# A streaming encoder layer on one core: VectorE's half of every split queued one step after ScalarE's, the spread product two steps behind its packing, the first FFN group loaded later

## The chip, the core and the metric

The kernel runs as one program on one core of a Trainium2 chip. The metric is the device time of one execution in microseconds (us); less is better. Before the change it is 1680.91 us, the median of three runs (1679.38 to 1682.36).

## The reference, cut to what matters

The reference is one layer of a hybrid encoder over 320 frames (256 of a prompt, 64 of a running stream that has 256 cached frames):

```python
xn = rmsnorm(x, norm_mix)
q, k, v, u, vs, g = split(xn @ w_in)          # 8 heads of 128; u, vs 1024 each; g 4096
a  = stick_breaking(q, k, v)                  # log-sigmoid, reversed cumulative sum, exp, @ v
bb = gelu(u) * (w_spatial . rmsnorm(gelu(vs)) + b_spatial)      # "SGU"
merged = sigmoid(g_a + b) * (a @ w_branch_a) + sigmoid(g_b + b) * (bb @ w_branch_b)
h  = x + merged @ w_out
hn = rmsnorm(h, norm_ffn)
h  = h + (silu(hn @ w_gate) * (hn @ w_up)) @ w_down             # 5632 hidden features
return rmsnorm(h, norm_final), k, v, vs
```

Everything is float32, and the weights (256 MB in all) are read once. A float32 product is made out of three matmuls of a high and a low part: high by high, high by low, low by high.

## The kernel before, in words

Features lie on the 128 partitions and the 320 frames on the free axis. A weight block of 128 output features is taken in steps of eight k-blocks, 24 matmuls a step (`product`, L98 to L100). After each step the code calls `tick()`, which counts the step and then calls everything that was registered for it with `at(tick, fn, rank)`, in the order of the ranks. So the program order of each engine's queue is written out by hand: TensorE, VectorE, ScalarE and SyncE run exactly what was emitted, in that order (`manual_schedule`), and only GpSimd's order is left to the framework. An instruction of VectorE that waits holds up all that stands behind it in VectorE's queue, whoever needs that.

Weights come in two schemes.

- `Plain` (six of the q/k/v heads, the 16 blocks of `w_out`, the first three gate/up pairs of the FFN): SyncE loads half a block (L115), ScalarE rounds it to fp32r (`high`, L120), VectorE subtracts (`low`, L123). The step `s` has its high at `s - 2` and its low at `s - 1`. The tiles: `raw` to `w`.
- `Group` (all other weights, in fp16, two steps to a unit): SyncE loads the raw block (L322); the largest magnitude of its rows is bounded by ScalarE (`junk`, L199, sum of magnitudes) or by VectorE (`tops`, L195, largest magnitude); VectorE packs it (`packed`, L207); TensorE spreads it over all partitions with one small product (`row`, L211), into the only buffer of its kind; VectorE makes the power of two from it (`close`: `peak`, `down`, `up`, L215 to L217, and `undo`, L342); ScalarE makes the high half (`w`, L349) and VectorE the low half (L352). The product of a unit starts at step `s`; its load is emitted at `s - lead`, the bound at `s - lead + 3`, the high at `s - 3`, the low at `s - 2`; with `last` the load step of the group's last unit, the packing comes at `last + 4`, the spreading at `last + 5`, the closing at `last + 6`. `lead` is 10 up to the out projection and 14 in the FFN.

Raw weights have five buffers (`RAW`), and four more (`raw2`) once the FFN begins; the `w` tiles have three (`SPLIT`). The small activation tiles rotate through 51 slots (`slot`, tile names `S`, `half`, `gate`, `act`).

The stages, with their times in the profile before: the first two q, k and v heads, with their loads (to 55 us); twelve Plain steps, four heads, in which the normalized input is made besides: VectorE multiplies `x` by the norm's factor (`normed`, L294), ScalarE makes its fp16 high half (`half`, L160) and VectorE the low half (L161) (to about 102 us); the fp16 heads, with the attention of four pairs of heads beside them, its small steps spread over twenty steps per pair by `attend` (to 330 us); the SGU, the gates and the branch products (to 640 us); the out projection (to 767 us); the FFN, in three slices, the first twelve steps Plain, which run while the norm of `h` is made and `ffn.normed` prepares 16 tiles as above (`mg`, L294; `half`, L160, L161); and from 1668 us the final norm and the stores. For the FFN's activations `gated` multiplies gate and up (L1029 to L1036), for its residual `downed` adds.

Splits of other activations are written the same way, ScalarE's copy at once followed by VectorE's subtraction in the same step: `gained` (L153, L154), `parts` in the attention (L593, L594), `merge` behind the branch products, and the softmax-like part of the attention (`att_soft`, L654 to L656, which loads ScalarE's function tables).

Of the kernel before, what the change touches and what calls it, by code (L numbers as in the profile page):

```python
# [22 lines left out]
H = 8  # L23
# [24 lines left out]
def stream_step(ctx: ExitStack, tc: tile.TileContext, xT, w_in, w_a, w_b, w_out, w_gu, w_down,  # L48
# [33 lines left out]

    rooms = {}
# [67 lines left out]
    def gained(src, gain, home=slot):  # L151
        hi, lo = home(), home()
        nc.scalar.activation(out=hi, in_=src, func=AF.Copy, scale=gain)  # L153
        nc.vector.scalar_tensor_tensor(out=lo, in0=src, scalar=gain, in1=hi.bitcast(F32),  # L154
                                       op0=ALU.mult, op1=ALU.subtract)
        return hi, lo

    def half(src, factor):
        x = slot((2, T), F16, "half")
        nc.scalar.activation(out=x[:, 0], in_=src, func=AF.Copy, scale=factor)  # L160
        nc.vector.scalar_tensor_tensor(out=x[:, 1], in0=src, scalar=factor, in1=x[:, 0], op0=ALU.mult, op1=ALU.subtract)  # L161
# [113 lines left out]
    class Features:  # L275
# [16 lines left out]
        def normed(self, m, src, factor, home=None):  # L292
            t = src if home is None else home
            nc.vector.tensor_tensor(out=t, in0=src, in1=got[factor], op=ALU.mult)  # L294
# [293 lines left out]
    def parts(src, engine=None):  # L588
# [5 lines left out]
        (engine or nc.vector).tensor_tensor(out=view(lo), in0=src, in1=view(hi.bitcast(F32)), op=ALU.subtract)  # L594
# [5 lines left out]
    def att_parts(p):  # L600
# [8 lines left out]
        nc.vector.tensor_tensor(out=own[:, :, 1], in0=new, in1=own[:, :, 0].bitcast(F32), op=ALU.subtract)  # L609
# [21 lines left out]
    def att_gather(p, part):  # L631
        s = attn[p]
        if part == 0:
# [5 lines left out]
            for j, r in enumerate(ROWS):  # L639
                nc.vector.tensor_tensor(out=z[0][r, Z:], in0=zs[j][r, TS : TS + PAST], in1=low[r, TS:], op=ALU.add)  # L640
                nc.vector.tensor_tensor(out=z[1][r, Z:], in0=zs[j][r, 0:TS], in1=low[r, 0:TS], op=ALU.add)
            nc.vector.tensor_tensor(out=z[1][:, Z:], in0=z[1][:, Z:], in1=mown, op=ALU.add)
# [50 lines left out]
    def att_join(p, what):  # L693
        s = attn[p]
        t = s[what]
        if what == "vt":
            av = s["av"] = rooms["late"].tile([P, 5 * P], F32, tag="av", name="av")
            together(av, t[0])
            s["ap"] = parts(av[:, 0 : 4 * P].rearrange("p (j d) -> p j d", j=2)[:, :, 0:P])
        else:  # L700
# [3 lines left out]
            s["tp"] = [parts(wt[:, j * 5 * P : j * 5 * P + TP]) for j in range(2)]  # L704

    def att_out(p):
# [15 lines left out]
        a = [slot(dt=F32, name="aT") for _ in range(2)]  # L722
        nc.scalar.copy(out=a[0], in_=po[0][:, 0:T])
        nc.scalar.copy(out=a[1][:, 0:TP], in_=po[1][:, 0:TP])
        nc.scalar.copy(out=a[1][:, TP:T], in_=po[0][:, T : T + TS])
        for t in a:
            aT.add(t)

# [476 lines left out]
```

## Time and profile before

| | |
|---|---|
| three runs, median | 1680.91 us (1679.38 to 1682.36) |
| profiled execution, its own time | 1682.18 us |
| its span in the profile | 1680.4 us |
| TensorE clock granted, mean | 0.985 |
| PE busy | 1615.0 us, 96% of the span |
| VectorE (DVE) busy | 1095.5 us, 65% |
| ScalarE (ACT) busy | 1009.1 us, 60% |
| GpSimd (POOL) busy | 57.3 us, 3% |
| read from HBM | 256.03 MB, 156 GB/s over the span |

The profile is one execution, recorded by the hardware. In its rows PE is TensorE, DVE VectorE, ACT ScalarE, SPq the DMA issues of SyncE; "L123" is line 123 of the kernel; "w<-raw" is a tile written and the tile read; a bracket holds the idle time of the engine just before an instruction and the instruction that ended it. PEclk is the clock granted to TensorE, 1.00 being full speed. Times are from the start of the span.

### The profile page before, as it was taken

The numbers are of one execution on the slowest core, as the hardware profiler recorded it, in microseconds if no ns is written. First come the engines' busy times: TensorE is split into PE (matmuls) and PEld (weight loads), VectorE is DVE, ScalarE is ACT, GpSimd is POOL, SyncE is SP. The second block draws the span as 40 slices with busy tenths as digits, with TensorE's granted clock in tenths as the row PEclk, the third lists the DMA queues.
The fourth block names the chain that finished last, engine by engine and source line by source line (L and its number), as shares of the span: only waits on it lengthen the run. The fifth ranks groups of instructions, "written<-read, shape, count | busy, mean of one in ns | idle before, by whom it ended". The sixth has DMA issues, their size and how long they took to land.

```text
span 1680.4 us, 28045 instructions
## 1 busy us (share of the span) xinstructions
PE 1615.0 (96%) x11692; PEld 1235.4 (74%) x11692; DVE 1095.5 (65%) x1819; ACT 1009.1 (60%) x1119; POOL 57.3 (3%) x80
## 2 busy tenths in 40 slices
PE   9979898999999999998599999999999999999997
PEld 9967666677777778998567777777777777777775
DVE  6678776786665565555565568765565686655775
ACT  6468888768766762444455657445555664555652
POOL 0110101100000000111000000000000000000000
PEclk9989999999999999999899999999999999999999
DMA  8556753564544444554444444544444444443331
GB/s 307 169 156 181 197 169 118 161 178 151 176 151 166 161 157 144 171 172 141 148 168 167 151 151 154 197 152 151 152 170 176 154 151 158 168 176 126 113 113 64
DMA packets 100512, 268.35 MB, mean 160 GB/s; under 512 B 28992, under 2 KB 35392, under 8 KB 100384
## 3 DMA queue, kind: packets, MB, share of 16 engines
q1 hardware_dynamic: 97936, 261.36, 46.7%
q0 software_dynamic: 1312, 3.80, 0.7%
q8 instruction: 91, 1.49, 0.4%
q10 hardware_dynamic: 1136, 1.39, 0.2%
q14 instruction: 37, 0.30, 0.1%
HBM read 256.03 MB, written 5.51 MB: 156 GB/s over the span
## 4 chain that ended last, share of the span: by engine, by line
PE 83%; DVE 7%; ACT 7%; DMA 2%; issue 2%; SPq 0%; ACTq 0%; DVEq 0%
PE acc L98 26%; PE acc L99 26%; PE acc L100 26%; DVE w L352 2%; PE aux L444 2%; ACT junk L199 1%; ACT w L349 1%; DMA raw<-w_gu 1%; DVE w L123 1%; PE acc L444 1%; ACT half L160 1%; PE row L211 1%; DMA raw<-w_in 1%; DVE tops L195 0%; DVE half L161 0%
## 5 line engine op out<-in xcount | busy, mean ns | idle before, releaser
L99 PE MATMUL acc<-half,w 128*128 128x320 f16 x3232 | 969.3, 300 | 0.0
L98 PE MATMUL acc<-half,w 128*128 128x320 f16 x3232 | 969.3, 300 | 0.0
L100 PE MATMUL acc<-half,w 128*128 128x320 f16 x3232 | 969.1, 300 | 0.0
L349 ACT ACTIVATE w<-raw,up 128x2048 f16<-128x2048 f32 (+1 forms) x206 | 405.6, 1969 | 413.6 <-PE acc L100 398.2
L352 DVE SCALAR_TENSOR_TENSOR w<-raw,up,w 128x2048 f16<-128x2048 f32 (+1 forms) x206 | 475.2, 2307 | 55.6 <-ACT w L349 55.0
L98 PEld LDWEIGHTS <-w 128*128 128x128 f16 x3232 | 317.1, 98 | 125.0 <-issue 1.3
L100 PEld LDWEIGHTS <-w 128*128 128x128 f16 x3232 | 317.1, 98 | 124.1
L99 PEld LDWEIGHTS <-w 128*128 128x128 f16 x3232 | 317.1, 98 | 118.4
L199 ACT ACTIVATE junk<-raw 128x2048 uint8<-128x2048 f32 (+1 forms) x149 | 277.8, 1865 | 8.5 <-DMA raw<-w_gu 8.5
L1036 DVE TENSOR_TENSOR act<-bb,ev 128x320 f32<-128x320 f32 x44 | 21.6, 492 | 171.9 <-ACT bb L1034 168.9
L195 DVE TENSOR_REDUCE tops<-raw 128x1 f32<-128x2048 f32 (+1 forms) x57 | 127.7, 2241 | 3.2 <-DMA raw<-w_gu 3.2
L215 DVE TENSOR_REDUCE peak<-row 128x1 f32<-128x128 f32 x148 | 42.3, 286 | 133.7 <-PE row L211 133.6
L120 ACT CAST w<-raw 128x1024 fp32r<-128x1024 f32 x56 | 58.7, 1047 | 82.4 <-PE acc L100 70.1
L123 DVE TENSOR_TENSOR w<-raw,w 128x1024 fp32r<-128x1024 f32 x56 | 77.7, 1390 | 14.1 <-ACT w L120 14.1
L98 PE MATMUL acc<-mh,w 128*128 128x320 f32 x256 | 79.3, 310 | 0.0
L99 PE MATMUL acc<-ml,w 128*128 128x320 f32 x256 | 79.1, 309 | 0.0
L100 PE MATMUL acc<-mh,w 128*128 128x320 f32 x256 | 79.1, 309 | 0.0
L211 PE MATMUL row<-turner,packed 128*128 128x128 bf16 x148 | 32.8, 222 | 41.4 <-DVE packed L207 40.2
L100 PE MATMUL acc<-S,w 128*128 128x320 f32 x144 | 47.6, 331 | 13.2 <-DVE w L123 13.2
L211 PEld LDWEIGHTS <-packed 128*128 128x128 bf16 x148 | 14.5, 98 | 50.6 <-DVE packed L207 45.4
L98 PEld LDWEIGHTS acc<-mh,w 128*128 128x128 f32 x256 | 48.1, 188 | 0.0
L99 PEld LDWEIGHTS acc<-ml,w 128*128 128x128 f32 x256 | 48.1, 188 | 0.0
(226 smaller groups left out, 1279.3 us busy)
## 6 DMA issues: line engine op xcount, KB each, us to landing
raw<-w_gu SPq DMA_DIRECT2D x176, 512.0 KB, 5.6
raw<-w_in SPq DMA_DIRECT2D x141, 512.0 KB, 4.8
raw<-w_down SPq DMA_DIRECT2D x80, 512.0 KB, 5.0
raw<-w_out SPq DMA_DIRECT2D x32, 512.0 KB, 3.9
raw<-w_a SPq DMA_DIRECT2D x16, 512.0 KB, 3.7
raw<-w_b SPq DMA_DIRECT2D x16, 512.0 KB, 4.6
raw<-w_down SPq DMA_DIRECT2D x16, 256.0 KB, 5.0
x<-xT SPq DMA_DIRECT2D x8, 320.0 KB, 7.5
```

The source lines that it names most:

```text
L98: nc.tensor.matmul(ps[:, :T], a, x[0], start=first, stop=False, skip_group_check=True)
L99: nc.tensor.matmul(ps[:, :T], a, x[1], start=False, stop=False, skip_group_check=True)
L100: nc.tensor.matmul(ps[:, :T], b, x[0], start=False, stop=last, skip_group_check=True)
L120: nc.scalar.copy(out=self.w[j][0], in_=self.raw[:, j * HALF * P : (j + 1) * HALF * P])
L123: nc.vector.tensor_tensor(out=self.w[j][1], in0=self.raw[:, j * HALF * P : (j + 1) * HALF * P], in1=self.w[j][0].bitcast(F32), op=ALU.subt ...
L195: nc.vector.tensor_reduce(out=self.tops[:, i : i + 1], in_=src, axis=mybir.AxisListType.X, op=ALU.max, apply_absolute_value=True)
L199: nc.scalar.activation(out=junk, in_=src, func=AF.Abs, accum_out=self.tops[:, i : i + 1])
L211: nc.tensor.matmul(self.row[:, :P], self.own.to_broadcast([P, P]), turner, start=True, stop=True)
L215: nc.vector.tensor_reduce(out=top, in_=self.row[:, :P], axis=mybir.AxisListType.X, op=ALU.max)
L349: nc.scalar.activation(out=w[:, 0], in_=self.raw[u][:, : self.width[u]], func=AF.Copy, scale=self.scale.up)
L352: nc.vector.scalar_tensor_tensor(out=self.w[u][1], in0=self.raw.pop(u)[:, : self.width[u]], scalar=self.scale.up, in1=self.w[u][0], op0=AL ...
L444: nc.tensor.matmul(first[b][h][:, :T], w[:, (h * n + j) * P : (h * n + j + 1) * P], xs[c + j][i], start=not last and c + j + i == 0, stop= ...
```

## The change

It changes the order in which the same instructions stand in the queues, and a few buffers.

- A helper `after(n, fn)` registers `fn` for `n` steps later. VectorE's part of a split (`half`, `gained`, `parts`, the own queries in `att_parts`, the sums of `att_gather`) is emitted one step after ScalarE's part, and a ScalarE part that needs a VectorE result is emitted one step after that: the `half` behind `normed`, the `parts` behind `av` and `wt` in `att_join`, the split planes behind `sgu_gain`, the copies behind `att_out`, the high and low of `merge`, `residual`, `gated` and the squares of `downed`. The last ones of a stage (the last three of 16) keep the old way.
- In `Group` the spreading comes at `last + 6` and the closing at `last + 7`. With `lead` 11 in place of 10 before the FFN, the load, the bound and the packing of a group stand one step earlier against its products, and the spreading and the closing where they stood. In the FFN the lead stays 14, so there the spreading and the closing stand one step nearer to the products; the first FFN group has lead 12, since the lead may not reach to before the FFN's first step (`min(14, now - ffn_start)`), so its loads stand behind later Plain loads.
- `normed` in the FFN gets six buffers of its own in the late pool in place of the one `mg` buffer; `merge` writes into a gate's tile. The SGU's four pairs of groups come every three steps in place of 10/3, and the output of the attention one step later.

Each engine has the same instructions, in the same number, in both kernels. The core of the diff (L numbers move by 6 or 7 up to `Group`, and by 14 and more behind the attention):

```diff
+    def after(n, fn, *a, rank=5):
+        if n == 0:
+            fn(*a)
+        else:
+            at(state["tick"] + n, fn, *a, rank=rank)
...
     def half(src, factor):
         x = slot((2, T), F16, "half")
         nc.scalar.activation(out=x[:, 0], in_=src, func=AF.Copy, scale=factor)
-        nc.vector.scalar_tensor_tensor(out=x[:, 1], in0=src, scalar=factor, in1=x[:, 0], op0=ALU.mult, op1=ALU.subtract)
+        after(1, lambda: nc.vector.scalar_tensor_tensor(out=x[:, 1], in0=src, scalar=factor, in1=x[:, 0],
+                                                        op0=ALU.mult, op1=ALU.subtract), rank=3)
...
-            t = src if home is None else home
+            t = src if home is None else home()
             nc.vector.tensor_tensor(out=t, in0=src, in1=got[factor], op=ALU.mult)
-            self.half.append(half(t, self.gain[:, m : m + 1]))
+            after(1, lambda: self.half.append(half(t, self.gain[:, m : m + 1])), rank=3)
...
             last = start + 2 * len(units) - 2 - lead
-            assert last + 6 <= start - 3
+            assert last + 7 <= start - 3
             at(last + 4, lambda: self.scale.pack(), rank=3)
-            at(last + 5, lambda: self.scale.spread(), rank=1)
-            at(last + 6, self.close, late_undo, rank=1)
+            at(last + 6, lambda: self.scale.spread(), rank=1)
+            at(last + 7, self.close, late_undo, rank=1)
...
-        (engine or nc.vector).tensor_tensor(out=view(lo), in0=src, in1=view(hi.bitcast(F32)), op=ALU.subtract)
+        after(wait, lambda: (engine or nc.vector).tensor_tensor(out=view(lo), in0=src, in1=view(hi.bitcast(F32)), op=ALU.subtract))
...
-            s["ap"] = parts(av[:, 0 : 4 * P].rearrange("p (j d) -> p j d", j=2)[:, :, 0:P])
+            after(1, lambda: s.update(ap=parts(av[:, 0 : 4 * P].rearrange("p (j d) -> p j d", j=2)[:, :, 0:P])))
...
-                groups[kind, s, i] = Group([pieces(w_gu[i], 0, KD), pieces(w_gu[KF + i], 0, KD)], now, lambda: [ffn.undo], 14, (1,) if made % 2 else ())
+                groups[kind, s, i] = Group([pieces(w_gu[i], 0, KD), pieces(w_gu[KF + i], 0, KD)], now, lambda: [ffn.undo], min(14, now - ffn_start), (1,) if made % 2 else ())
...
-        at(base + 3 + m // 2, lambda m=m: ffn.normed(m, hs[m], "rh", t320("mg", 1)))
+        at(base + 3 + m // 2, lambda m=m: ffn.normed(m, hs[m], "rh", lambda: rooms["raw"].tile([P, T], F32, tag="normed", bufs=6, name="normed")))
```

How the queues change is seen at three places. The first is VectorE's queue in the twelve Plain steps; `x` is the input being normalized, `half` its fp16 halves, `w` the weights' low half, `k` a head. Before:

```order
L123 TENSOR_TENSOR w<-raw,w 128x1024
L743 TENSOR_TENSOR k<-acc,rx 128x320
L294 TENSOR_TENSOR x<-x,rx 128x320
L161 SCALAR_TENSOR_TENSOR half<-x,gain_608,half 128x320
L294 TENSOR_TENSOR x<-x,rx 128x320
L161 SCALAR_TENSOR_TENSOR half<-x,gain_608,half 128x320
L123 TENSOR_TENSOR w<-raw,w 128x1024
```

and in the changed kernel, from the same product of a `k` head on:

```order
L757 TENSOR_TENSOR k<-acc,rx 128x320
L301 TENSOR_TENSOR x<-x,rx 128x320 x2
L129 TENSOR_TENSOR w<-raw,w 128x1024
L167 SCALAR_TENSOR_TENSOR half<-x,gain_608,half 128x320 x2
L301 TENSOR_TENSOR x<-x,rx 128x320 x2
L129 TENSOR_TENSOR w<-raw,w 128x1024
```

The two `half` of a step no longer stand directly behind the `x` from which ScalarE has to make their high halves: there is a `w`, a step's worth of ScalarE's time, between them.

The second place is VectorE's queue at the beginning of the fp16 heads, where the attention's first `parts` (`S`) fall; `packed` is the packing of the next group. Before:

```order
L215 TENSOR_REDUCE peak<-row 128x1
L216 TENSOR_TENSOR down<-peak,bits 128x1
L217 TENSOR_TENSOR up<-down,bits 128x1
L342 TENSOR_SCALAR undo<-down,undo_610 128x1
L352 SCALAR_TENSOR_TENSOR w<-raw,up,w 128x2048
L207 TENSOR_SCALAR packed<-tops 128x1
L743 TENSOR_TENSOR v<-acc,rx 128x320
L215 TENSOR_REDUCE peak<-row 128x1
```

and in the changed kernel:

```order
L359 SCALAR_TENSOR_TENSOR w<-raw,up,w 128x2048
L601 TENSOR_TENSOR S<-q,S 128x256
L601 TENSOR_TENSOR S<-k,S 128x256 x2
L616 TENSOR_TENSOR S<-q,S 128x2x64
L757 TENSOR_TENSOR v<-acc,rx 128x320
L214 TENSOR_SCALAR packed<-tops 128x1
L222 TENSOR_REDUCE peak<-row 128x1
L223 TENSOR_TENSOR down<-peak,bits 128x1
```

In the kernel before, the `peak` behind a `packed` belongs to the same group, and the spreading product that reads `packed` stands in the very next step of TensorE's queue; in the changed kernel the `peak` is that of the group ahead, and the spreading product stands two steps behind its `packed`. The `S` have moved away from ScalarE's copies by a step as well.

The third place is SyncE's queue at the FFN's start, with the buffers' numbers; in the piece before, `raw_8504` and `raw_8575` are the two units of the first FFN group, `raw_8664` the first of the second, and `raw_8573` and `raw_8662` Plain blocks:

```order
L115 DMA raw_8502<-w_gu 128x1024
L322 DMA raw_8504<-w_gu 128x1024
L115 DMA raw_8573<-w_gu 128x1024
L322 DMA raw_8575<-w_gu 128x1024
L115 DMA raw_8662<-w_gu 128x1024
L322 DMA raw_8664<-w_gu 128x1024
```

and in the changed kernel, where `raw_8556`, `raw_8643` and `raw_8645` are these three units and `raw_8554` and `raw_8641` the Plain blocks:

```order
L121 DMA raw_8486<-w_gu 128x1024
L121 DMA raw_8554<-w_gu 128x1024
L329 DMA raw_8556<-w_gu 128x1024
L121 DMA raw_8641<-w_gu 128x1024
L329 DMA raw_8643<-w_gu 128x1024
L329 DMA raw_8645<-w_gu 128x1024
```

The first group's first unit stands one Plain block later against the Plain loads (beside `raw_8554`, the fifth of six blocks, where it stood beside `raw_8502`, the fourth), and the last Plain block stands ahead of that group's second unit, where it stood behind it.

More of the change, by code (lines that the diff above doesn't have):

```diff
@@ L586, in att_rows, with parts @@
                                                    in_=cv[:, :, 2 * p * P : (2 * p + 2) * P]))
-    def parts(src, engine=None):
+    def parts(src, engine=None, wait=1):
         n = src.free_size()
@@ L608, in att_parts @@
         nc.scalar.copy(out=own[:, :, 0], in_=new)
-        nc.vector.tensor_tensor(out=own[:, :, 1], in0=new, in1=own[:, :, 0].bitcast(F32), op=ALU.subtract)
+        after(1, lambda: nc.vector.tensor_tensor(out=own[:, :, 1], in0=new, in1=own[:, :, 0].bitcast(F32), op=ALU.subtract))
     def att_past(p):
@@ L638, in att_gather, with add @@
                 nc.scalar.copy(out=low[r, :], in_=zs[j][ROWS[1 - j], 0:T])
[L639 to L642, printed above, removed]
+            def add():
+                for j, r in enumerate(ROWS):
+                    nc.vector.tensor_tensor(out=z[0][r, Z:], in0=zs[j][r, TS : TS + PAST], in1=low[r, TS:], op=ALU.add)
+                    nc.vector.tensor_tensor(out=z[1][r, Z:], in0=zs[j][r, 0:TS], in1=low[r, 0:TS], op=ALU.add)
+                nc.vector.tensor_tensor(out=z[1][:, Z:], in0=z[1][:, Z:], in1=mown, op=ALU.add)
+            after(1, add)
             return
@@ L703, in att_join @@
             together(wt[:, 5 * P :], t[1])
-            s["tp"] = [parts(wt[:, j * 5 * P : j * 5 * P + TP]) for j in range(2)]
+            after(1, lambda: s.update(tp=[parts(wt[:, j * 5 * P : j * 5 * P + TP]) for j in range(2)]))
     def att_out(p):
@@ L721, in att_out, with out @@
             mm(po[j][:, P:TP], av[:, (2 * j + 1) * P : (2 * j + 2) * P], w[:, TP:], False, True)
[L722 to L727, printed above, removed]
+        def out():
+            a = [slot(dt=F32, name="aT") for _ in range(2)]
+            nc.scalar.copy(out=a[0], in_=po[0][:, 0:T])
+            nc.scalar.copy(out=a[1][:, 0:TP], in_=po[1][:, 0:TP])
+            nc.scalar.copy(out=a[1][:, TP:T], in_=po[0][:, T : T + TS])
+            after(1, lambda: [aT.add(t) for t in a])
+        after(1, out)
     aT, bT = Acts(H), Acts(H)
@@ L884, in sgu_gain, with split @@
             nc.gpsimd.dma_start(out=sv_t[g], in_=own[:, j * TS : (j + 1) * TS])
-        y = vplane[p] = planes("vsp", 5 * P)
-        for j in range(2):
-            apart(y[:, :, j * TP : (j + 1) * TP], vs[2 * p + j][:, 0:TP])
-        apart(y[:, :, 4 * P :], own)
+        def split():
+            y = vplane[p] = planes("vsp", 5 * P)
+            for j in range(2):
+                apart(y[:, :, j * TP : (j + 1) * TP], vs[2 * p + j][:, 0:TP])
+            apart(y[:, :, 4 * P :], own)
+        after(1, split)
     def sgu_turn(p):
@@ L905, in sgu_mix, with out @@
                              start=True, stop=True)
-        for j in range(2):
+        def out(j):
             g = 2 * p + j
@@ L916, in sgu_mix @@
             bT.add(r)
+        for j in range(2):
+            after(1, out, j)
     at(base + 4, sgu_norm)
     for p in range(4):
-        step = base + 10 * p // 3
+        step = base + 3 * p
         at(step + 5, sgu_gain, p)
         at(step + 7, sgu_turn, p)
-        at(step + 10, sgu_join, p)
-        at(step + 12, sgu_mix, p)
+        at(step + 9, sgu_join, p)
+        at(step + 11, sgu_mix, p)
     for g in range(H):
@@ L996, in stream_step, with residual, more @@
     sq = Squares("sq_h")
-    def residual(m, ps, x):
+    def residual(m, ps, x, wait):
         nc.vector.tensor_tensor(out=hs[m], in0=ps, in1=x, op=ALU.add)
-        hg.append(gained(hs[m], g_ffn[:, m : m + 1]))
-        sq.add(hs[m], nc.vector if m == KD - 1 else None)
+        def more():
+            hg.append(gained(hs[m], g_ffn[:, m : m + 1], wait=wait))
+            sq.add(hs[m], nc.vector if m == KD - 1 else None)
+        after(wait, more)
     for m in range(KD):
@@ L1007, in stream_step @@
         if m < KD - 1:
[L1008 removed]
+            after(1, residual, m, ps, x, m < KD - 3, rank=2)
         else:
[L1010 removed]
+            residual(m, ps, x, 0)
     mctx.close()
```

49 lines of the change are left out of this document (29 added, 20 removed).

## The prediction

> **What bounds the kernel now.** I read the stages first: the span cut where the weights' scheme changes (from, to, length; busy time and instructions of PE, PEld, DVE, ACT, POOL; PEclk; DMA share; GB/s).
>
> ```profile
> 55.00:112.00 57.00, 44.97 (x276) 42.40 (x275) 42.27 (x77) 33.61 (x46) 9.80 (x14) 0.88 0.50 159
> 112.00:330.00 218.00, 199.81 (x1455) 144.79 (x1454) 163.51 (x314) 179.55 (x238) 20.41 (x24) 0.98 0.59 167
> 330.00:640.00 310.00, 309.54 (x2315) 224.83 (x2312) 207.87 (x415) 207.54 (x222) 3.24 (x6) 1.00 0.49 163
> 640.00:767.00 127.00, 127.00 (x876) 122.91 (x874) 71.29 (x88) 49.75 (x68) 12.37 (x14) 1.00 0.50 160
> 767.00:850.00 83.00, 58.43 (x345) 54.15 (x344) 51.22 (x87) 39.04 (x51) 4.03 (x1) 0.88 0.42 143
> 850.00:1660.00 810.00, 810.00 (x6003) 584.50 (x6002) 515.52 (x760) 463.00 (x437) 0.00 (x0) 1.00 0.43 151
> ```
>
> TensorE is busy all but 0.46 us at full clock from 330 to 767 and from 850 to 1660 us: a new order can win nothing there. (Before 55 us, the loads, and after 1660, the final norm, nothing is reordered but the squares.) It idles, at a lower clock, in three stages: 55 to 112 (12.03 us idle), 112 to 330 (18.19) and 767 to 850 (24.57). Next, two undisturbed stretches of PE alone give the price of a matmul when nothing waits:
>
> ```profile
> 880.00:1000.00 120.00, 120.00 (x891) 1.00 0.48 167
> 690.00:750.00 60.00, 60.00 (x412) 1.00 0.53 172
> ```
>
> That is 120/891 = 0.1347 us in fp16 and 60/412 = 0.1456 us in the Plain scheme. At these prices the three stages need 276 x 0.1456 = 40.2, 1455 x 0.1347 = 196.0 and 345 x 0.1456 = 50.2 us. So they lose 57 - 40.2 = 16.8, 218 - 196.0 = 22.0 and 83 - 50.2 = 32.8 us, 71.6 together. Third, who TensorE waits for, one fence for each of the three stages (us in total, times, longest):
>
> ```profile
> PE row L211 <- DVE packed L207: 10.6, 3, 7.0
> ```
>
> ```profile
> PE row L211 <- DVE packed L207: 17.0, 9, 2.9
> ```
>
> ```profile
> PE acc L100 <- DVE w L123: 12.5, 2, 8.0
> PE row L211 <- DVE packed L207: 12.1, 3, 4.9
> ```
>
> These are the longest of each stage. All of it is VectorE being late, mostly with `packed`, which is itself short (0.15 us, below): what counts is what stands ahead of it.
>
> **Part 1, the Plain steps (55 to 112).** VectorE's timeline over one step:
>
> ```profile
> 61.12 1.22 DVE L123 TENSOR_TENSOR w<-raw,w 128x1024 fp32r<-128x1024 f32 x1
> ...
> 63.77 0.55 DVE L161 SCALAR_TENSOR_TENSOR half<-x,gain,half 128x320 f16<-128x320 f32 x1 [0.63 <-ACT half L160]
> 64.24 0.48 DVE L294 TENSOR_TENSOR x<-x,rx 128x320 f32<-128x320 f32 x1
> 65.36 0.55 DVE L161 SCALAR_TENSOR_TENSOR half<-x,gain,half 128x320 f16<-128x320 f32 x1 [0.63 <-ACT half L160]
> 65.83 1.22 DVE L123 TENSOR_TENSOR w<-raw,w 128x1024 fp32r<-128x1024 f32 x1
> ```
>
> From one `w` to the next are 4.71 us, and TensorE's step is 24 x 0.1456 = 3.49 us: here VectorE sets the pace, because twice a step it waits for ScalarE's half of a tile that it has itself only just made. In the change those two instructions stand a step later. Without the two waits of 0.63 us the step is 4.71 - 1.26 = 3.45 us, just under TensorE's, and less where no head's output is written. So `w` and `packed` fall no further behind from step to step. What may still be late is a first `packed`; I leave 1 of the 16.8 us and take 15.8. The cover is thin, 0.04 us a step in one step of two: if ScalarE's halves were late again by 0.3 us each, 2 x 0.3 - 0.04 = 0.56 us a step, over some ten steps 5 to 6 us, would stay.
>
> **Part 2, the fp16 heads (112 to 330).** The chain, from the timelines of VectorE and then of TensorE:
>
> ```profile
> 193.03 2.35 DVE L352 SCALAR_TENSOR_TENSOR w<-raw,up,w 128x2048 f16<-128x2048 f32 x1 [3.82 <-ACT w L349]
> 195.29 0.15 DVE L207 TENSOR_SCALAR packed<-tops 128x1 bf16<-128x1 f32 x1
> ```
>
> ```profile
> 195.50 0.23 PE L211 MATMUL row<-turner,packed 128*128 128x128 bf16 x1 [2.39 <-DVE packed L207]
> ```
>
> ScalarE is late with a group's high half, VectorE's low half waits 3.82 us for it, `packed` of another group stands behind that, and TensorE's spread product, in the next step, waits 2.39 us in the middle of products whose weights are ready. The low half is not late for its own product: the list of waits has none for it. So the wait costs TensorE because pack and spread are one step apart. In the change they are two, 24 x 0.1347 = 3.2 us more, against a longest wait of 2.9 us in the rows above: taken by itself that already covers every wait of this stage. The second half of the part is ScalarE's own lateness:
>
> ```profile
> 222.22 0.74 ACT L656 ACTIVATE e<-e 128x640 f32<-128x640 f32 x1
> 222.86 1.99 ACT L349 ACTIVATE w<-raw,up 128x2048 f16<-128x2048 f32 x1
> ...
> 230.60 0.41 ACT L593 CAST S<-av 128x256 fp32r<-128x256 f32 x1 [3.44 <-DVE av L574]
> ...
> 231.63 2.00 ACT L349 ACTIVATE w<-raw,up 128x2048 f16<-128x2048 f32 x1
> ```
>
> The second high half comes 231.63 - 222.86 = 8.8 us after the first, a group's products take 48 x 0.1347 = 6.5, and 3.44 of the 8.8 is a wait for VectorE's `av`. The change queues this cast a step behind `av`, so it no longer waits. A burst of attention work stays. A high half can start when the product three groups back has freed its buffer, two groups or 12.9 us before its own product; with 2.0 for it and 2.35 for the low half, ScalarE may be 12.9 - 4.4 = 8.5 us late. The longest ScalarE work that the new order puts between two high halves I add up from such rows to an estimated 13 us; less the group's 6.5 that is 6.5 late, within 8.5. ScalarE's 179.55 us busy are 92% of the 196.0 that TensorE needs. I leave 2 of the 22.0 and take 20.
>
> A rule bears on the clock's share of that. The 3.4 us behind the spread product of 195.50, in the columns of PE alone:
>
> ```profile
> 196.20:199.60 3.40, 3.40 (x15) 0.51 0.87 192
> ```
>
> After 2.39 us of idle time the clock is halved (0.51) for 3.4 us. The Trainium skill, "TensorE: Matmul & The Clock Gate" (What's actually happening), lets the clock fall only after at least one idle window of about 3.4 us. By that rule the 199.81 - 196.0 = 3.8 us of slow matmuls in this stage, whose waits are all shorter, would come from elsewhere and stay, and the gain would be about 4 us less. The trace disagrees: 2.4 us of idle time do it.
>
> With the clock counted as the rows show it, these 3.8 us go with the idle time.
>
> **Part 3, the FFN's start (767 to 850).** SyncE's queue, ScalarE's, then VectorE's:
>
> ```profile
> 775.40 0.33 SPq L322 DMA_DIRECT2D raw<-w_gu  x1
> 775.78 1.09 SPq L115 DMA_DIRECT2D raw<-w_gu  x1
> 776.92 0.42 SPq L322 DMA_DIRECT2D raw<-w_gu  x1
> 789.58 0.33 SPq L115 DMA_DIRECT2D raw<-w_gu  x1
> ```
>
> ```profile
> 801.03 1.91 ACT L199 ACTIVATE junk<-raw 128x2048 uint8<-128x2048 f32 x1 [5.83 <-DMA raw<-w_gu]
> ```
>
> ```profile
> 777.98 0.51 DVE L247 STREAM_TRANSPOSE rh<-root 128x320 f32<-128x320 f32 x1 [2.61 <-ACT root L245]
> ...
> 782.81 2.29 DVE L195 TENSOR_REDUCE tops<-raw 128x1 f32<-128x2048 f32 x1 [3.22 <-DMA raw<-w_gu]
> 803.52 0.55 DVE L161 SCALAR_TENSOR_TENSOR half<-mg,gain,half 128x320 f16<-128x320 f32 x1 [6.87 <-ACT half L160]
> ```
>
> From 776.92 to 789.58 SyncE's queue stands, because a Plain load (L115) waits for a buffer, and with it the second group's loads behind it. ScalarE then waits 5.83 us for that raw block, its `half` stands behind that, VectorE waits 6.87 us for the `half`, and `w` and `packed` stand behind that: TensorE's stop of 8.0. In the new order this last Plain block takes a free buffer of the late pool; the first group's second unit waits for the buffer that came free at 775.40, and the second group's loads stand right behind it. They come 10 us earlier or more, and the 5.83 go. The 3.22 of VectorE go because that bound stands two steps later, 2 x 3.49 us. The halves stand two steps later and in six `normed` buffers, so neither engine waits inside a pair.
>
> What is late next is VectorE itself. From the norm's result (`rh`), at 778.5, it has about 8 `w` (1.22), 16 products and 16 halves (0.48 + 0.55 = 1.03), one `tops` (2.29) and two `gated` (about 1.9 each, estimated as four such rows): 9.8 + 16.5 + 2.3 + 3.9 = 32.5 us, and the first low half of a group 2.35. TensorE's twelve steps end 12 x 3.49 = 41.9 us after 767, at 809, which leaves 30.5, and the last halves are only needed near the end of the first unit, 6 us on. That is about even; I leave 3 of the 32.8 and take 29.8. The spread and the close, a step nearer to the products in the FFN, cost nothing later on: from 850 to 1660 PE never waits and DVE is 64% busy (515.52 of 810).
>
> **The other edits.** `merge`, `residual`, `sgu_mix`, `downed` and the moved GpSimd loads fall into stages in which PE was full before: they can gain nothing, and cost something only if a result comes later than its reader's step; the rows of 330 to 767 and 850 to 1660 say how much room there is (DVE 67%, 56%, 64% busy). Nothing, then, with 3 us as the bound (one step late). After 1668 us nothing moves: the last three blocks keep the old order.
>
> **Sum.** 15.8 + 20 + 29.8 = 65.6. The profiled execution took 1682.18 us (span 1680.4), 1.27 above the median; the gain is the same for both: 1682.2 - 65.6 = 1616.6 there, 1680.9 - 65.6 = 1615.3, rounded 1615, for the median.
>
> **The rivals.**
>
> *ScalarE's bursts still stop TensorE* in the second stage: if the estimated 13 us between two high halves is 15 or more, every pair of heads stalls it, and 15 of the 22.0 us stay in place of 2: 1615 + 13 = 1628. For it: ACT 92% busy. Against it: its waits of 3.4 us go. Chance 0.13.
>
> *The FFN's start stays bound by VectorE or the loads*: half of the 32.8 us stays, 16.4 in place of 3: 1628. For it: my sum comes out about even. Chance 0.17. Both together: 1641, 0.04.
>
> *The change does not take hold*, since the new places fill with other waits of the same kind: about 1681, 0.04.
>
> *Slower: the loads.* The bound stands a step earlier, but its load cannot, since it waits for one of five raw buffers:
>
> ```profile
> 192.40 0.58 SPq L322 DMA_DIRECT2D raw<-w_in  x1
> ```
>
> ```profile
> 202.61 1.90 ACT L199 ACTIVATE junk<-raw 128x2048 uint8<-128x2048 f32 x1
> ```
>
> ```profile
> raw<-w_in SPq DMA_DIRECT2D x141, 512.0 KB, 4.8
> ```
>
> From issue to bound are 10.2 us at a tight place; a step less leaves 7.0, and a landing takes 4.8. It is slower from a landing of about 9.7 us on: ScalarE has 196.0 - 179.55 = 16.5 us to spare over some 30 groups (1455/48), 0.5 each, and 66/30 = 2.2 us of wait more for each eat up the whole gain, 7.0 + 0.5 + 2.2. At 10 us it would be 1615 + 30 x 2.5 = 1690. Against it: ScalarE waits nowhere for `w_in` before. Chance 0.04.
>
> **How the numbers follow.** The forecast has 0.58. The low end is all 71.6 us gone, 1609, less 5, because attention's matmuls have fewer than 320 columns and are priced too high in 196.0: 1604. The high end holds each of the two likelier rivals with two thirds of their loss and a late step in place of half, and nearly their sum: 1640. Out of the range are both together, no effect and slower: 0.12. A measurement can tell about 0.2%, 3.4 us, from no change. Faster 0.92, same 0.04, slower 0.04.
>
> **What would show it.** Right: PEclk 1.00 and no wait for `packed` over 1 us in 55 to 330; no 0.63 us waits before `half`; a `w` every 3.5 us; group loads by 778 us at the FFN's start; the last matmul near 1605. Wrong: ScalarE waiting for `raw<-w_in` (the loads), gaps of TensorE behind `w` L356 (the bursts), or VectorE without idle time from 778 to 815 us with TensorE waiting for it.

## The result, and the profile after

The changed kernel takes 1623.4 us, median of four runs (1620.54 to 1624.51), beside 1680.49 for the kernel before, measured beside it: a ratio of 0.9657 with a 95% interval of 0.964 to 0.9673, 57 us less. The forecast was 1615, with a range of 1604 to 1640; the gain forecast was 65.6, so 8 us of it are missing. The profiled execution (1620.54 us, the fastest of the four; span 1618.7) stands against a forecast of 1616.6.

The same windows of the changed kernel (from, to, length; busy time of PE, PEld, DVE, ACT, POOL; PEclk; DMA share; GB/s). The work in a window is not the same, since later stages begin up to 62 us earlier; the FFN begins near 738 us now.

```profile
55.00:112.00 57.00, 51.94 (x352) 47.07 (x351) 51.59 (x98) 40.20 (x56) 8.70 (x14) 0.94 0.61 193
112.00:330.00 218.00, 214.94 (x1602) 159.15 (x1601) 179.99 (x344) 190.55 (x252) 28.12 (x28) 0.99 0.63 181
330.00:640.00 310.00, 309.49 (x2299) 228.37 (x2297) 196.04 (x391) 196.25 (x208) 1.82 (x2) 1.00 0.48 159
640.00:767.00 127.00, 127.00 (x869) 126.80 (x867) 74.84 (x102) 62.79 (x90) 18.88 (x15) 1.00 0.60 194
767.00:850.00 83.00, 82.04 (x600) 62.50 (x599) 58.55 (x93) 53.17 (x54) 0.00 (x0) 1.00 0.49 172
```

In these windows the idle time of TensorE was 12.0, 18.2 and 24.6 us in the three stages that waited; it is 5.1, 3.1 and 1.0. To compare the same work, I cut the changed kernel where TensorE starts the same matmul into `acc`, counted from the first, at which the three stages begin and end in the kernel before. They are there 57.0, 217.9 and 83.1 us long, and here:

```profile
55.07:100.73 45.66, 40.60 (x277) 38.87 (x275) 42.58 (x82) 33.16 (x48) 8.70 (x14) 0.95 0.59 192
100.73:300.01 199.28, 196.43 (x1452) 145.19 (x1452) 161.00 (x302) 177.78 (x234) 25.98 (x24) 0.99 0.64 183
737.55:788.42 50.87, 49.91 (x346) 47.41 (x345) 45.19 (x81) 35.71 (x49) 4.03 (x1) 1.00 0.70 238
```

So the stages are 11.4, 18.6 and 32.2 us shorter. All of TensorE's waits for VectorE, in the whole span, are now these (us in total, times, longest; the names are those of the changed kernel's lines, L218 the spread, L222 `peak`, L629 the attention's first score product, L721 its output); its other waits add up to 1.6 us:

```profile
PE aux L629 <- DVE S L616: 5.1, 1, 5.1
PE row L218 <- DVE peak L222: 1.5, 3, 0.8
PE aux L721 <- DVE S L601: 1.3, 1, 1.3
PE acc L105 <- DVE half L167: 1.0, 1, 1.0
```

No wait for `packed` is left. VectorE's timeline in the Plain steps has lost its two waits, and in the step shown a `w` comes 2.9 us after the other, where it took 4.7; on average over the eight that end the stage it is 3.6 us, where it was 4.9:

```profile
61.05 1.22 DVE L129 TENSOR_TENSOR w<-raw,w 128x1024 fp32r<-128x1024 f32 x1
62.19 1.00 DVE L167 SCALAR_TENSOR_TENSOR half<-x,gain,half 128x320 f16<-128x320 f32 x2
63.11 0.88 DVE L301 TENSOR_TENSOR x<-x,rx 128x320 f32<-128x320 f32 x2
63.91 1.22 DVE L129 TENSOR_TENSOR w<-raw,w 128x1024 fp32r<-128x1024 f32 x1
```

What is new is one stop of 5.06 us, in front of the attention's first score product. VectorE's timeline ahead of it, and then TensorE's:

```profile
92.54 0.16 DVE L223 TENSOR_TENSOR down<-peak,bits 128x1 int32<-128x1 int32 x1
92.74 3.11 DVE L224 TENSOR_TENSOR up<-down,bits 128x1 int32<-128x1 int32 x1
95.77 0.20 DVE L349 TENSOR_SCALAR undo<-down,undo 128x1 f32<-128x1 f32 x1
95.89 2.33 DVE L359 SCALAR_TENSOR_TENSOR w<-raw,up,w 128x2048 f16<-128x2048 f32 x1
98.15 0.41 DVE L601 TENSOR_TENSOR S<-q,S 128x256 fp32r<-128x256 f32 x1
98.49 0.74 DVE L601 TENSOR_TENSOR S<-k,S 128x256 fp32r<-128x256 f32 x2
99.16 0.28 DVE L616 TENSOR_TENSOR S<-q,S 128x128 fp32r<-128x128 f32 x1
```

```profile
99.49 0.90 PE L629 MATMUL aux<-S 128*128 128x320 f32 x2 [5.06 <-DVE S L616]
```

VectorE works without a gap here, but the own queries' split (`S`, L616) was moved one step back and its reader was not: the score product stands one step behind it where it stood two. An instruction of 0.16 us besides took 3.11. From 2.0 us into the stop on, the clock is halved for 6.8 us:

```profile
96.40:103.20 6.80, 3.71 (x14) 0.50 0.51 167
```

So this one place costs 5.1 us, and half of the 3.7 us of products in the slow stretch: about 7 in all, some of it behind 100.73 us, in the next stage.

### The profile page after: what moved, and what is told of

Its sections match the earlier page's. It is cut to its first block, busy times and chain, and to the rows that moved or that the text cites. A ratio compares the mean times of both kernels' runs of the same rounds, so it can differ in the third digit from the quotient of the medians.

```text
span 1618.7 us, 28003 instructions
## 1 busy us (share of the span) xinstructions
PE 1598.7 (99%) x11692; PEld 1225.4 (76%) x11692; DVE 1089.1 (67%) x1819; ACT 1004.5 (62%) x1119; POOL 65.3 (4%) x80
## 4 chain that ended last, share of the span: by engine, by line
PE 86%; ACT 6%; DVE 5%; issue 2%; DMA 1%; SPq 0%; DVEq 0%; ACTq 0%
PE acc L105 27%; PE acc L104 27%; PE acc L106 27%; PE aux L451 2%; ACT w L356 1%; ACT junk L206 1%; DVE w L359 1%; DMA raw<-w_in 1%; DVE tops L202 1%; PE acc L451 1%; DVE half L167 1%; DVE w L129 0%; PE row L218 0%; DMA turned<-wp 0%; DVE wt L581 0%
## 5 line engine op out<-in xcount | busy, mean ns | idle before, releaser
L222 DVE TENSOR_REDUCE peak<-row 128x1 f32<-128x128 f32 x148 | 42.6, 288 | 182.3 <-PE row L218 182.2
L129 DVE TENSOR_TENSOR w<-raw,w 128x1024 fp32r<-128x1024 f32 x56 | 68.8, 1232 | 50.3 <-ACT w L126 50.3
L104 PEld LDWEIGHTS acc<-mh,w 128*128 128x128 f32 x256 | 48.1, 188 | 0.0
L106 PEld LDWEIGHTS acc<-mh,w 128*128 128x128 f32 x256 | 48.0, 188 | 0.0
L104 PE MATMUL acc<-S,w 128*128 128x320 f32 x144 | 44.7, 310 | 0.0
L106 PE MATMUL acc<-S,w 128*128 128x320 f32 x144 | 44.5, 309 | 0.0
L105 PE MATMUL acc<-S,w 128*128 128x320 f32 x144 | 44.5, 309 | 0.0
```

The costliest lines, as they stand in the source:

```text
L104: nc.tensor.matmul(ps[:, :T], a, x[0], start=first, stop=False, skip_group_check=True)
L105: nc.tensor.matmul(ps[:, :T], a, x[1], start=False, stop=False, skip_group_check=True)
L106: nc.tensor.matmul(ps[:, :T], b, x[0], start=False, stop=last, skip_group_check=True)
L129: nc.vector.tensor_tensor(out=self.w[j][1], in0=self.raw[:, j * HALF * P : (j + 1) * HALF * P], in1=self.w[j][0].bitcast(F32), op=ALU.subt ...
L222: nc.vector.tensor_reduce(out=top, in_=self.row[:, :P], axis=mybir.AxisListType.X, op=ALU.max)
```

## The experiments

The theory going in: three stages with three causes (VectorE's and ScalarE's turns at one tile in the Plain steps; late ScalarE and a spread one step behind the packing in the fp16 heads; the order of the loads at the FFN's start). Rivals: one of the parts does it all. In the first two runs one half of the change is taken alone.

**The spread alone, in the kernel before.**

```diff
-            at(last + 5, lambda: self.scale.spread(), rank=1)
-            at(last + 6, self.close, late_undo, rank=1)
+            at(last + 6, lambda: self.scale.spread(), rank=1)
+            at(last + 7, self.close, late_undo, rank=1)
...
-            g = Group([[(w_a[n], H), (w_b[n], H)]], start, lambda: [aT.undo, bT.undo], 10, (0,) if n % 3 == 2 else (), True)
+            g = Group([[(w_a[n], H), (w_b[n], H)]], start, lambda: [aT.undo, bT.undo], 11, (0,) if n % 3 == 2 else (), True)
```

(and the lead of the `w_in` groups likewise)

> The kernel before, with only the spread product and the closing one step later and lead 11 before the FFN; every VectorE half stays in the step of ScalarE's. My theory (three stages with three causes): only the stage 112 to 330 gains, about 18 of its 22 us, because two steps between packing and spread cover waits of up to 2.9 us; VectorE still needs 4.7 us a step from 55 to 102, so that stage keeps at least 12 of its 16.8 us, and the FFN's start keeps its 32.8: about 1663 us. Rival (one cause): TensorE waits almost only for packed, so distance from packed to spread is the whole gain: about 1627 us.

Measured: 1671.93 us (1670.2 to 1673.09), ratio 0.995 (0.9936 to 0.9965). Both expectations fail: 9 us, and not from where either said. By the same cut the Plain steps are 5.7 us shorter and the FFN's start 7.1, which were to keep all or most of their loss, and the fp16 heads, which were to gain 18, are 2.5 us longer. The window 112 to 330, and TensorE's waits in it:

```profile
112.00:330.00 218.00, 195.77 (x1436) 142.01 (x1434) 165.45 (x318) 180.34 (x240) 20.41 (x24) 0.98 0.61 170
```

```profile
PE row L211 <- DVE peak L215: 15.6, 9, 4.8
PE aux L622 <- DVE packed L207: 4.8, 2, 2.4
```

TensorE idles 22.2 us there, no less than the 18.2 of before. The wait for `packed` has turned into one for `peak`, that of the group ahead, which has to read the only `row` buffer before the next spread may write it. (The kernel before has one such wait there, of 1.2 us.) Close comes one step behind spread and the next spread one step behind that: the distance taken from `packed` to the spread leaves just as little between `peak` and the next spread.

**The delays alone.** The other half: the changed kernel with the numbers of the run above set back, and `min(14, now - ffn_start)` left.

```diff
-            at(last + 6, lambda: self.scale.spread(), rank=1)
-            at(last + 7, self.close, late_undo, rank=1)
+            at(last + 5, lambda: self.scale.spread(), rank=1)
+            at(last + 6, self.close, late_undo, rank=1)
```

> The changed kernel with the spread one step behind the packing again and lead 10 (all VectorE halves stay a step later; the first FFN group keeps min(14, distance)). My theory: the stages 55 to 112 and 767 to 850 keep their gain (together about 41 us by the profile after), and 112 to 330 keeps part of it because ScalarE no longer waits for av and wt: 5 to 17 us of packed waits come back there, about 1630 to 1640 us. Rival (one cause, the distance to the spread): about 1680 us.

Measured: 1618.73 us (1616.89 to 1622.16), ratio 0.9637 (0.9621 to 0.9653): all of the gain, and some 5 us more than the changed kernel has, though the intervals overlap a little. The stages 112 to 330 and 767 to 850:

```profile
112.00:330.00 218.00, 216.31 (x1627) 160.24 (x1625) 183.71 (x360) 193.09 (x256) 25.20 (x30) 1.00 0.65 186
767.00:850.00 83.00, 79.35 (x583) 59.70 (x583) 55.11 (x85) 51.29 (x50) 0.00 (x0) 1.00 0.47 163
```

Only 1.7 us idle in the fp16 heads; one stop of 3.65 us, for `packed`, is at the FFN's start. My 1630 to 1640 us missed as well: of the waits for `packed` only these 1.7 us came back in the heads, not 5 to 17. The rival (distance does it) is dead, and with the run before so is my statement that two steps by themselves cover the stage.

**The halves at once.** In the changed kernel:

```diff
-        after(1, lambda: nc.vector.scalar_tensor_tensor(out=x[:, 1], in0=src, scalar=factor, in1=x[:, 0],
+        after(0, lambda: nc.vector.scalar_tensor_tensor(out=x[:, 1], in0=src, scalar=factor, in1=x[:, 0],
...
-            after(1, lambda: self.half.append(half(t, self.gain[:, m : m + 1])), rank=3)
+            after(0, lambda: self.half.append(half(t, self.gain[:, m : m + 1])), rank=3)
```

> The changed kernel with half and normed written at once again: ScalarE's half directly behind VectorE's product, VectorE's half directly behind that; all else as changed. My theory: VectorE waits 0.63 us before each half again, its step from 60 to 102 is longer than TensorE's, 10 to 15 us come back there, and 5 to 15 at the FFN's start: 1638 to 1652 us. Rival: the two steps of distance hide that too: within 3 us of 1623.

Measured: 1645.56 us (1643.56 to 1648.9), ratio 0.979 (0.9774 to 0.9807): 22 us come back, as expected. The windows of the three stages, and VectorE's timeline with the old wait in it:

```profile
55.00:112.00 57.00, 45.78 (x284) 41.64 (x284) 44.98 (x83) 34.62 (x49) 10.96 (x14) 0.94 0.52 169
112.00:330.00 218.00, 211.51 (x1579) 156.08 (x1578) 174.15 (x336) 190.12 (x250) 27.07 (x26) 1.00 0.65 179
767.00:850.00 83.00, 70.58 (x472) 56.14 (x471) 57.00 (x94) 48.12 (x52) 0.00 (x0) 0.96 0.48 167
```

```profile
63.61 0.55 DVE L167 SCALAR_TENSOR_TENSOR half<-x,gain,half 128x320 f16<-128x320 f32 x1 [0.63 <-ACT half L166]
```

TensorE idles 11.2 and 12.4 us in the first and the last of them again; 112 to 330 idles 6.5, so these two edits do little for the fp16 heads.

**The first FFN group's loads as before.** In the changed kernel:

```diff
- ... lambda: [ffn.undo], min(14, now - ffn_start), (1,) if made % 2 else ())
+ ... lambda: [ffn.undo], 14, (1,) if made % 2 else ())
```

> The changed kernel with lead 14 for the first FFN group too, so that its loads stand where they stood before the change. My theory: SyncE's queue stands behind a Plain load that waits for a buffer again, ScalarE waits over 4 us for a raw block near 800 us and TensorE stops behind it: 10 to 25 us come back, 1633 to 1648 us. Rival: the gain at the FFN's start is from the halves and the six normed buffers, and the order of the loads costs nothing: within 3 us of 1623.

Measured: 1628.19 us (1627.71 to 1629.34), ratio 0.9692 (0.9678 to 0.9706). It costs 4 to 5 us by the medians (4.8 beside the 1623.4, 3.8 beside the repeat below), under my 10 and over the rival's 3; in the trace the FFN's start is 7.7 us longer. ScalarE's wait for the raw block is back, longer than it was before the change:

```profile
768.44 1.91 ACT L206 ACTIVATE junk<-raw 128x2048 uint8<-128x2048 f32 x1 [6.32 <-DMA raw<-w_gu]
```

but TensorE does not wait 6 us for it. All its waits from 745 to 850 us:

```profile
PE acc L106 <- DVE w L129: 3.3, 2, 2.6
PE acc L105 <- DVE half L167: 1.8, 1, 1.8
PE acc L104 <- ACT w L126: 1.1, 1, 1.1
```

With the halves apart, most of a late load is covered by the steps in between.

**The changed kernel again, and the stop near 94 us.** Four kernels on one chip: the changed one, each of these two edits, and both.

```diff
-    at(base + 10, att_past, 0)
+    at(base + 7, att_past, 0)
...
-    attend(0, base + 10)
+    attend(0, base + 11)
```

> The changed kernel again, as the base for the three kernels beside it on the same chip: 1620 to 1625 us, with TensorE's stop of 5 us near 94 us in front of the attention's first score product.

> The changed kernel with the first pair's attention steps all one step later (attend of pair 0 from base + 11), all else the same. My theory: the stop of 5.1 us near 94 us comes from the delayed own-query split standing only one step ahead of the score product; a step more (3.5 us) takes 3.5 to 5 us of it away, and up to 3.4 us of half clock: 4 to 8 us less than the changed kernel. Rival: VectorE is full from 78 to 100 us, so TensorE stops the same time for the next thing that VectorE is late with: no difference.

> The changed kernel with the split of the first pair's cached keys (att_past 0, which has GpSimd's three subtractions) three steps earlier. My theory: VectorE's up took 3.11 us in place of 0.16 because GpSimd worked at that time; moved to another place it holds VectorE where there is room, and the stop near 94 us shrinks by about 3 us: 2 to 5 us less than the changed kernel. Rival: GpSimd holds VectorE by the same time wherever it stands and VectorE has no room: no difference.

> Both edits of the two kernels before this one. My theory: the stop near 94 us is gone with its half clock: 5 to 9 us less than the changed kernel, about 1615 us. Rival: VectorE full, no difference.

Measured: 1624.43 us (ratio 0.9666, 0.9652 to 0.9679); with the attention a step later 1618.94 (0.9633, 0.962 to 0.9646); with the cached keys early 1621.05 (0.9645, 0.9632 to 0.9658); both 1620.12 (0.964, 0.9626 to 0.9653). The step of distance takes 5.5 us off, its interval clear of the first's. In the window around the stop, the changed kernel as first profiled and then the one with the attention later:

```profile
78.00:100.00 22.00, 16.94 (x117) 15.51 (x116) 21.86 (x39) 17.26 (x26) 4.82 (x7) 0.92 0.51 164
```

```profile
78.00:100.00 22.00, 21.41 (x151) 18.65 (x150) 21.77 (x43) 17.85 (x27) 6.08 (x8) 1.00 0.58 182
```

VectorE is as full in both; TensorE's stop is 0.59 us in place of 5.06. VectorE's split of the own queries and TensorE's score product, with the attention later:

```profile
97.90 0.28 DVE L616 TENSOR_TENSOR S<-q,S 128x128 fp32r<-128x128 f32 x1
98.24 0.85 PE L629 MATMUL aux<-S 128*128 128x320 f32 x4 [0.59 <-DVE S L616]
```

TensorE comes to the product 3.2 us later (at 97.65, where it was 94.43), and the split ends 1.3 us earlier (98.18 for 99.44): together the 4.5 us. The first is the place in the queue. The second goes with GpSimd's subtractions, which the edit moved too: `up` took 0.16 us in this run. So the two causes went together, and the queue's place has the larger share. Both kernels with the attention later have a stop of 2.7 us near 136 us instead, for another S of L616; I didn't look into it.

The early keys moved only one of the three GpSimd subtractions (the other two belong to the second pair, which I had overlooked when I wrote the expectation), and `up` was held 2.21 us in place of 3.11. The stop was 4.2 us in that profile, 0.9 less than 5.06, so in this trace TensorE's stop shrinks by as much as `up` does; in the repeated kernel it was 5.25. But the 3.4 us less in time are not clear of the interval, and on top of the other edit the early keys gave nothing; how much GpSimd costs of the whole stays open.

**The attention's splits at once.** In the changed kernel, `parts`, the own queries, the gather's sums, both parts of `att_join` and the copies of the output without their delay:

```diff
-    def parts(src, engine=None, wait=1):
+    def parts(src, engine=None, wait=0):
...
-            after(1, lambda: s.update(tp=[parts(wt[:, j * 5 * P : j * 5 * P + TP]) for j in range(2)]))
+            after(0, lambda: s.update(tp=[parts(wt[:, j * 5 * P : j * 5 * P + TP]) for j in range(2)]))
...
-        at(now + 19, att_out, p)
+        at(now + 18, att_out, p)
```

> The changed kernel with the attention's splits written at once again (parts, own queries, the sums of the gather, the copies behind the output); half, normed, spread and loads stay as changed. My theory after the first runs: the stage 112 to 330 is won by these delays, since ScalarE waits for av and wt again without them (15 us in the profile before) and everything queued behind is late: 8 to 18 us come back there, while the stop near 94 us (5 us) goes: 1628 to 1637 us. Rival: the stage was won by the order of the halves and of the packing, and these delays cost only the stop near 94 us: about 1618 us.

Measured: 1638.73 us (1636.13 to 1639.98), ratio 0.9748 (0.9734 to 0.9761): 14 to 15 us come back, a little over my range. All of it, and more, is in the fp16 heads; by the same cut they take 220.0 us, while the Plain steps are 4.5 us shorter, since the stop near 94 us is gone. Below, the window, then ScalarE's waits in it, then TensorE's:

```profile
112.00:330.00 218.00, 197.24 (x1439) 143.24 (x1437) 166.40 (x314) 180.22 (x240) 21.53 (x26) 0.98 0.60 166
```

```profile
ACT S L600 <- DVE av L581: 9.8, 4, 3.3
ACT S L600 <- DVE wt L581: 7.3, 2, 7.1
```

```profile
PE row L218 <- DVE peak L222: 14.2, 8, 3.9
PE aux L629 <- DVE packed L214: 4.8, 2, 2.4
```

20.8 us idle, about as in the kernel before (18.2), although halves, spread and loads are as changed. So the attention's delays are what that stage's gain hangs on. ScalarE waits 17 us for `av` and `wt` here (15.5 in the kernel before, never in the changed one), and VectorE for ScalarE; that it is these two, of the delays taken back together, is argued from the waits and not taken apart.

**More room for the spread.** Two kernels, on top of the spread alone: four places in the one `row` buffer, then every second spread in a buffer of the attention's pool.

```diff
-            self.row = aux1()
+            self.row = rows[:, state["row"] % 4 * P : (state["row"] % 4 + 1) * P]
...
-            self.row = aux1()
+            self.row = aux() if state["row"] % 2 and "raw" not in rooms else aux1()
```

> The kernel with only the spread moved (e1), and four places in the PSUM buffer of the spread product in place of one, so that a spread product no longer waits for the closing of the group ahead. My theory: the distance gained nothing from 112 to 330 because the wait went from packed to the peak of the group ahead, which holds the only row buffer and stands behind the same late instruction of VectorE; without that the 15.6 us of waits for peak go, and e1's 1672 becomes 1655 to 1660. Rival: VectorE is late as such, and the next thing (a low half, a score product) stops TensorE as long: within 4 us of 1672.

> The kernel with only the spread moved (e1), and every second spread product of the stages before the FFN in a PSUM buffer of the attention's pool (aux) in place of the one row buffer. In e1 and with four places in one buffer the spread product was still released by the peak of the group ahead, over 5 us after its own packed. My theory: two buffers take that wait away; the 15 us of waits for peak between 112 and 330 fall to under 5, part of it comes back as other waits for VectorE, and the time falls by 6 to 12 us from e1's 1672 to 1660 to 1666. Rival: VectorE is late as such and TensorE waits as long for its next result: within 4 us of 1672.

Measured: 1669.75 us (ratio 0.9934, 0.9922 to 0.9947) and 1673.69 (0.9957, 0.9944 to 0.9971), beside 1671.93 (0.995) without. The first halved the waits for `peak` in the window, from 15.6 us to 7.0, and did not take them away: the spread still ran when the other group's `peak` was done, 5.7 us after its own `packed`. VectorE, then TensorE:

```profile
267.18 0.16 DVE L207 TENSOR_SCALAR packed<-tops 128x1 bf16<-128x1 f32 x1 [1.27 <-ACT junk L199]
...
271.91 0.82 DVE L663 SCALAR_TENSOR_TENSOR e<-z,e 128x640 f32<-128x640 f32 x1 [2.81 <-ACT e L658]
272.65 0.28 DVE L216 TENSOR_REDUCE peak<-row 128x1 f32<-128x128 f32 x1
```

```profile
272.99 0.22 PE L212 MATMUL row<-turner,packed 128*128 128x128 bf16 x1 [2.00 <-DVE peak L216]
```

The second did. The longest of TensorE's waits from 112 to 330 with two buffers:

```profile
PE aux L711 <- DVE z L649: 5.8, 2, 4.1
PE aux L212 <- DVE packed L207: 4.9, 1, 4.9
```

None is for `peak`, and the time is the same. The rival holds: VectorE is late as such, and TensorE waits as long for whatever comes out of its queue next. ScalarE still waits 17 us for `av` and `wt` in both kernels, as with the spread alone. (The 5.8 us for `z` are partly the price of sharing the attention's buffers, so this run doesn't say what two buffers of its own would give.)

**A version faster than both.** Delays as changed; the spread one step behind the packing and lead 10 before the FFN, two steps in the FFN; the first pair's attention one step later.

```diff
-            at(last + 6, lambda: self.scale.spread(), rank=1)
-            at(last + 7, self.close, late_undo, rank=1)
+            far = lead > 10
+            at(last + 5 + far, lambda: self.scale.spread(), rank=1)
+            at(last + 6 + far, self.close, late_undo, rank=1)
...
-    attend(0, base + 10)
+    attend(0, base + 11)
```

> The changed kernel with the spread one step behind the packing and lead 10 again before the FFN, two steps in the FFN, and the first pair's attention one step later. If the delays are the whole gain and the distance of the spread costs something before the FFN: no stop over 2 us near 94 and near 780 us, 1612 to 1617 us. Rival: one step of distance is too little beside the moved attention, and packed waits come back: 1618 to 1624 us.

Measured: 1615.01 us (1614.33 to 1615.89), ratio 0.9609 (0.9596 to 0.9622), 8 to 9 us less than the changed kernel, intervals apart, and inside the 1612 to 1617 us of the expectation. From the kernel with only the attention later (1618.94) it differs by the spread and the lead before the FFN alone. So there the second step of distance seems to cost time: by the same cut the heads take 197.6 us here and 196.7 with the delays alone, the two kernels with one step, and 199.3 to 203.7 in the seven traces that have the attention's delays and two. TensorE's waits for VectorE over 0.4 us in the whole span:

```profile
PE row L218 <- DVE packed L214: 5.6, 5, 1.7
PE acc L105 <- DVE half L167: 1.0, 1, 1.0
```

**Stage by stage.** The traces of the main runs, all cut at the same matmuls into `acc`; us:

| kernel | Plain steps | fp16 heads | FFN's start |
|---|---|---|---|
| before | 57.0 | 217.9 | 83.1 |
| changed | 45.7 | 199.3 | 50.9 |
| changed, repeated | 45.9 | 203.7 | 51.8 |
| the spread alone | 51.3 | 220.4 | 76.0 |
| the delays alone | 44.0 | 196.7 | 53.9 |
| halves at once | 54.9 | 202.0 | 65.5 |
| first FFN group's loads as before | 45.8 | 199.3 | 58.6 |
| attention's splits at once | 41.2 | 220.0 | 50.9 |
| attention later | 39.2 | 203.3 | 51.1 |
| faster than both | 40.8 | 197.6 | 50.9 |

With nothing changed, two executions differ by 4.4 us in the heads; a smaller difference there says nothing by itself.

## Why the prediction was right, and where it was not

*What bounds the kernel.* Right. The three stages were the place: TensorE's idle time and half clock went there and nowhere else, and the stages that were full stayed full (437.5 us from the heads' end to the FFN, where they took 437.0).

*Part 1, the Plain steps.* The mechanism was right: with the halves at once again, the old waits of 0.63 us and 11.2 us of idle time return. The step that failed is "what may still be late is a first `packed`; I leave 1". What was late was the attention's first score product, whose operand was moved back a step and which itself was not. 5.1 us of idle time and a half clock stayed, about 7 us; one step more for the attention took 5.5 of them away. The prediction went over VectorE's queue and not over the readers of what the change delays. By the same work the stage gained 11.4 us, not 15.8.

*Part 2, the fp16 heads.* The size came out close: by the same work 18.6 us of the 20 booked, though only 14.2 in the repeated kernel's trace. But the step "taken by itself that already covers every wait of this stage" (two steps from pack to spread) failed outright. Alone, the distance leaves 22.2 us idle, since the next spread waits for the `peak` of the group ahead in the only `row` buffer, which the prediction left out of the account; a second buffer takes that wait and not the time. Beside the delays the second step seems to cost time before the FFN, as the fastest version shows. The other half of the part, ScalarE's waits for `av` and `wt`, which I had as an addition, is all of it that shows: with the attention's delays taken back, 20.8 us of idle time return; without the distance, 1.7 remain. I was right on the sum by luck, counting two causes for one loss.

*Part 3, the FFN's start.* 3 us booked to stay, about 1 did: 32.2 us gained for 29.8. The size was right; the loads, from which the part starts, were not the largest cause. With the halves apart, their order is worth 7.7 us of this stage, and the halves 14.6. The remainder, with the six `normed` buffers that the delay needs, wasn't taken apart. That VectorE's sum would come out "about even" was too dark: TensorE waits 1.0 us for it.

*The other edits.* No stage that was full lost more than 0.5 us.

*The rivals.* ScalarE's bursts did not stop TensorE; neither half of the FFN's loss nor "no effect" came. Of the slower rival, the loads, there is a trace: ScalarE's `junk` waits 1.7 us for `w_in` now, which it never did before (its 8.5 us of waits were for `w_gu`). That is 1.7 us in all, where the rival needed 2.2 us in each of some 30 groups:

```profile
L206 ACT ACTIVATE junk<-raw 128x2048 uint8<-128x2048 f32 (+1 forms) x149 | 278.0, 1866 | 1.7 <-DMA raw<-w_in 1.7
```

*The sum.* In the profiled execution 11.4 + 18.6 + 32.2 = 62.2 us were gained where 65.6 were booked, less 0.5 in the stages between: 3.9 us short (4.4 too few in Part 1, 1.4 in Part 2, 2.4 more than booked in Part 3). The median misses 8, because the profiled execution is the fastest of its four and the one before was 1.7 us above its median.

## What to carry to other kernels

When two engines write halves of one tile in turns, put a step's worth of other work between the halves: an instruction that waits at the head of an in-order queue delays everything behind it, and the engine that appears to wait (here TensorE, for `packed`) can be only the last victim. Before widening the distance in front of that victim, ask what the next wait on the same queue would be; a wait that only changes its name has not been covered. And when an operand moves a step back, move its reader or count the steps that are left.

## What the runs showed of the hardware

*VectorE is held while GpSimd works, over several of its instructions.* `up`, of 0.16 us, took 3.11, from 92.74 to 95.85 us. It began 0.6 us ahead of three subtractions that GpSimd ran back to back, while GpSimd issued a DMA, and ended with the last of them. GpSimd's timeline:

```profile
92.05 1.26 POOL L535 DMA_DIRECT2D wso<-ws_t  x2 [0.29 <-POOL wso L528]
93.32 2.50 POOL L601 TENSOR_TENSOR S<-k,S 128x320 fp32r<-128x320 f32 x3
```

The Trainium skill, "SBUF — State Buffer" (SBUF: two separate sides), has the two engines share a pair of ports as an exclusive lock, with VectorE blocked if its instruction has two SBUF inputs and GpSimd reads SBUF. The trace agrees (`down` and `bits` are two such inputs), and shows that a tiny instruction can wait for three GpSimd subtractions in a row, not for one; in the repeated kernel it was `down`, of 0.16 us, that took 3.09 beside the same three.

*The clock.* The Trainium skill, "TensorE: Matmul & The Clock Gate" (What's actually happening), asks for an idle window of about 3.4 us before the clock falls. In the stop of 5.06 us here the clock fell 2.0 us after TensorE's last work, and stayed at half for 6.8 us. In the kernel before, the half clock came behind a stop of 2.39 us at 193 us and did not come behind another of 2.39 us at 243 us (PEclk 1.00 from 245.3 to 252); in the kernel with the delays alone, a stop of 3.65 us at the FFN's start was followed by none (PEclk 1.00). So the measurements differ from that rule, and the length of a stop alone does not tell; the prediction's "2.4 us of idle time do it" is too general as well.
